# Laying out SBUF pools so that tiles read by TensorE begin at multiples of 2 KB

## The chip, the cores and the metric

One core of a Trainium2 chip runs the whole program. The metric is the device time of one execution in microseconds (us). TensorE (PE) does the matmuls, with its weight loads shown apart (PEld); VectorE (DVE), ScalarE (ACT) and GpSimd (POOL) do the elementwise work; SyncE (SP) issues the DMAs.

## The reference, cut to what matters

Two decoder layers over 512 positions of width 1024, all in float32. Layer 0 mixes positions by trailing means, layer 1 by differential attention over keys and values shared from the stream behind layer 0. Both end in a gated feed-forward network with a causal convolution of three taps:

```
for i in (0, 1):
    if i == 0: x = x + multiscale_pool(rmsnorm(x, norm_g[0, 0]), pool_w, pool_scale)
    else:
        k, v = rmsnorm(x, kv_norm) @ w_kv          # 1024 x (1024 + 1024)
        x = x + diff_attention(rmsnorm(x, norm_g[1, 0]), wq, lam, subln_g, wo, k, v)
    u = causal_dwconv(rmsnorm(x, norm_g[i, 1]) @ w_up[i], conv_w[i], conv_b[i])   # 1024 x 5632
    a, g = split(u)
    x = x + (silu(g) * a) @ w_down[i]              # 2816 x 1024
return rmsnorm(x, final_norm)
```

The two feed-forward networks are the bulk of it.

## The kernel before, in words

Every large product keeps float32 accuracy by splitting both operands into a high part (rounded to the type float32r) and a low part (the rest), and adding three matmuls of 128 x 128 weights: high by high, high by low, low by high. This is `mm3`, lines 158, 159 and 160, so each product shows as three lines of the profile. In a matmul the stationary operand (the 128 columns that are loaded as weights) is named second in a row of the trace, the moving operand (the 128, 256 or 512 columns that stream through) first: `pu<-n1h,hi_u` streams `n1h` through weights `hi_u`.

The products, by the name of their PSUM tile:

- `pu`, the up product of a feed-forward network: stationary a 128-column slice of a weight chunk (`hi_u`, `lo_u`), moving 512 positions of the normed and transposed stream (`n1h`, `n1l`; `n3h`, `n3l` in layer 1). The first four chunks of each layer are done in two halves of 256 positions each.
- `pd`, the down product: stationary a slice of the activations (`ah`, `al`), moving half a weight chunk (`hi_d`, `lo_d`).
- `pv`, the values: stationary the stream `n2`, moving half a weight chunk. `pw`, the output projection: stationary the heads' output, moving half a weight chunk.
- `pj_q`, `pj_k`, queries and keys: stationary a slice of a weight chunk, moving the stream `n2`.
- `pp`, the pooling maps: stationary the differences (`dhi`, `dlo`), moving 256 columns of a pooling weight.
- `sc`, `po`, `pa`, `pt`, `dps`: scores, weighted values, transposes and pooling bands.

SBUF is cut into pools that lie end to end in the order in which they are opened: `const` (residual stream `x`, gains, identity), `wp` (weight chunks: 3 raw, 5 high, 5 low buffers of 4 KB per partition), `work` (scratch, small vectors, loaded rows), `hp` (the normed stream, two buffers of 16 KB), `tp` (44 buffers of 2 KB: bands, pooling weights, activations, queries, keys, values). Where a pool begins is thus set by the sizes of those before it. In the built program the tiles that TensorE reads begin at these offsets from a multiple of 2048 bytes in their partition:

| tiles | before |
|---|---|
| `wp`: weight chunks, raw, high and low | 1984 |
| `hp`: `n1`, `n2`, `n3`, high and low | 1536 |
| `tp`: bands, pooling weights, `d`, `ah`, `al`, queries, keys, values, heads' output | 1536 |
| `work`: `aT`, `on` (2 KB scratch) | 1152 |
| `work`: `e`, `sq` (4 KB wide tiles) | 960 |
| `const`: identity | 1152 |

A slice adds its own start: 512 bytes for each 128 columns, 2048 for each 512. So a moving slice of `pu` begins at 1536, one of `pd` at 1984, and a stationary slice of `pu` 64 bytes ahead of a multiple of 512.

The instructions of TensorE stand in the order of the code (a manual schedule), and those of the other compute engines of the first 60 us too; `ORDER` is that list of steps. SP loads weight chunks ahead, as far as the raw buffers are free. `rows` loads a vector as rows of 128 into a tile of tag `vrow` (6 buffers), and `columns` turns them by a transpose on PE and a copy on DVE; step `c` of `ORDER` does that for the kv gain, the sub-norm gain and layer 0's convolution.

Of the kernel before, what the change touches and what calls it, by code (L numbers as in the profile page):

```python
# [8 lines left out]
F32 = mybir.dt.float32  # L9
# [5 lines left out]
P = 128  # L15
# [3 lines left out]
KD = D // P  # L19
# [44 lines left out]
def trunk(ctx, tc, x, norm_g, pool_w, pool_scale, kv_norm, w_kv, wq, lam, subln_g, wo,  # L64
          w_up, conv_w, conv_b, w_down, final_norm, consts, out):
    nc = tc.nc
    const = ctx.enter_context(tc.tile_pool(name="const", bufs=1))
    wp = ctx.enter_context(tc.tile_pool(name="wp", bufs=1))
    work = ctx.enter_context(tc.tile_pool(name="work", bufs=1))
    hp = ctx.enter_context(tc.tile_pool(name="hp", bufs=1))  # L70
    tp = ctx.enter_context(tc.tile_pool(name="tp", bufs=1))
    psum = ctx.enter_context(tc.tile_pool(name="psum", bufs=8, space=bass.MemoryType.PSUM))
    ctx.enter_context(tc.manual_schedule(engines={mybir.EngineType.PE}))

    def bank(name):
        return psum.tile([P, S], F32, tag="ps", name=name)
# [29 lines left out]
    nc.gpsimd.memset(halfneg, -0.5)  # L106

    def rows(src, n, name):
        r = work.tile([P, P], F32, tag="vrow", bufs=6, name=f"r_{name}")
        nc.sync.dma_start(out=r[:n, :], in_=src)  # L110
        return r, n, name

# [5 lines left out]
        return halves  # L118


    ones = const.tile([P, P], F32, name="ones")
    nc.vector.memset(ones, 1.0)

    def warm(n):
# [4 lines left out]
    load_x(0)  # L129
    nc.sync.dma_start(out=ident, in_=consts[:, :P])  # L130
    gn_rows = rows(norm_g.rearrange("l i (k p) -> (l i k) p", p=P), 4 * KD, "gn")
    nc.sync.dma_start(out=bands[0], in_=consts[:, P + S:P + 2 * S])
    load_x(1)
# [31 lines left out]
    def columns(loaded):  # L165

        r, n, name = loaded
        ps = bank(f"pv_{name}")
        nc.tensor.transpose(ps[:, :n], r[:n, :], ident[:n, :n])
        c = const.tile([P, n], F32, name=f"c_{name}")  # L170
        nc.vector.tensor_copy(c, ps[:, :n])
        return c
# [27 lines left out]
    class Normed:  # L200
# [13 lines left out]
        def vectors(self, t):  # L214
            self.rms(t)
            self.scale(t)
# [20 lines left out]
    def up_chunk(l, m):  # L237
        return chunk(w_up[l, :, m * P:(m + 1) * P].rearrange("(k p) c -> p k c", p=P), KD, P, f"u{l}_{m}")
# [6 lines left out]
    def conv_rows(l):  # L245
        return ([rows(conv_w[l, i].rearrange("(m p) -> m p", p=P), 2 * NF, f"cw{l}{i}") for i in range(3)]
                + [rows(conv_b[l].rearrange("(m p) -> m p", p=P), 2 * NF, f"cb{l}")])
# [12 lines left out]
    load_x(3)  # L260
    n1 = Normed("n1", across(norm_g[0, 1], "g1"))
    up0 = [up_chunk(0, (n + 1) % 2 * NF + n // 2) for n in range(2 * EARLY)]
    vec_rows = [rows(kv_norm.rearrange("(k p) -> k p", p=P), KD, "gkv"), rows(subln_g, 1, "gsub")]
    cw_rows = conv_rows(0)

    gn, shared, cw0 = [], [], []
# [75 lines left out]
        product(0, n, pup[n], up0[n][1:], n1, 0, S // 2)  # L342

    def vectors(_):
        shared.extend(columns(r) for r in vec_rows)
        cw0.extend(columns(r) for r in cw_rows)


# [1 line left out]
    steps = dict(a=pool_rms, h=pool_scaled, g=gains, m=pool_weights, x=pool_weights_split, i=pool_in,  # L350
                 s=pool_split, o=pool_out, r=pool_add, q=n1.rms, v=n1.scale, t=n1.turn, u=n1.split,
                 H=up_high, L=up_low, p=up_product, c=vectors, W=warm)
    with tc.manual_schedule(engines={mybir.EngineType.PE, mybir.EngineType.Activation,
                                     mybir.EngineType.DVE, mybir.EngineType.Pool}):
# [69 lines left out]
    def to_n2(t, dh):  # L424
# [3 lines left out]
        if t > 1:  # L428
# [2 lines left out]
    ffn(0, n1, cw0, [w[1:] for w in up0], pup, to_n2)  # L431


    gkv, gsub = shared
    gq = gn[0][:, 2 * KD:3 * KD]
    nc.vector.tensor_scalar(gsub, gsub, 1.0 - LAM_INIT, None, ALU.mult)
    lamt = scratch("lamt")
# [1 line left out]
                      in_=lam.rearrange("l a b -> l (a b)").to_broadcast([P, 4 * HD]))  # L439
# [318 lines left out]
```

## Time and profile before

| what | value |
|---|---|
| runs | 1019.69, 1019.77, 1018.54 us; median 1019.69 |
| profiled execution | 1019.51 us, its span 1017.7 us |
| PE busy | 1003.3 us, 99% |
| DVE busy, ACT busy | 56%, 42% |
| DMA | mean 94 GB/s, 8 tenths busy in the first fortieth of the span, 4 or less in all others |
| granted clock of TensorE | 0.998 of full speed over the span |

A matmul's time in a row is that of its passage through the engine; in the timeline the next begins before it ends. What a stream of matmuls costs is the distance from one start to the next, read from the timeline of PE.

### The profile page before, as it was taken

What the parts mean: (1) busy time and instruction counts of PE and PEld (TensorE: products, weight loads), DVE (VectorE), ACT (ScalarE), POOL (GpSimd) and SP (SyncE); (2) the same over time, 40 slices, a digit from 0 to 9 for tenths busy, and PEclk for the clock granted to TensorE, in tenths of its full rate; (3) what the DMA queues carried; (4) which work ended last, traced back from release to release, by engine and by line L of the source; (5) the groups of instructions that cost most, each with busy time, mean ns of one, the idle gap of its engine ahead of it and who ended that gap; (6) DMA issues with size and microseconds to landing.
All of it is one profiled execution on the core that took longest, in us unless ns stands there. A gap on an engine that the chain in (4) does not pass through costs nothing.

```text
span 1017.7 us, 12343 instructions
## 1 busy us (share of the span) xinstructions
PE 1003.3 (99%) x4871; PEld 835.6 (82%) x4871; DVE 569.5 (56%) x873; ACT 427.1 (42%) x671; POOL 86.1 (8%) x113
## 2 busy tenths in 40 slices
PE   8999999999999999999999999999999999999997
PEld 7998888888888888878888887988888888888885
DVE  5766656656632223457866797675665665622213
ACT  5554444443431213446756662454344443421311
POOL 3500000000000001261220101000000000000001
PEclk9999999999999999999999999999999999999999
DMA  8333333233232321243213111243333233232212
GB/s 256 108 104 104 90 97 103 85 102 104 83 109 84 113 88 57 79 129 104 63 42 104 63 43 42 83 125 104 91 96 104 85 102 104 83 104 85 102 42 82
DMA packets 128707, 95.33 MB, mean 94 GB/s; under 512 B 3329, under 2 KB 111498, under 8 KB 128650
## 3 DMA queue, kind: packets, MB, share of 16 engines
q1 hardware_dynamic: 128650, 94.55, 30.3%
q8 instruction: 38, 0.62, 0.3%
q14 instruction: 19, 0.16, 0.0%
HBM read 92.44 MB, written 2.10 MB: 93 GB/s over the span
## 4 chain that ended last, share of the span: by engine, by line
PE 97%; DVE 1%; DMA 1%; issue 0%; SPq 0%; ACT 0%; DVEq 0%; POOLq 0%; POOL 0%; ACTq 0%
PE pu L158 16%; PE pu L159 16%; PE pu L160 16%; PE pd L160 8%; PE pd L158 8%; PE pd L159 8%; PE sc L527 2%; PE po L556 2%; PE pw L160 1%; PE pv L158 1%; PE pv L160 1%; PE pv L159 1%; PE pj_k L159 1%; PE pj_k L158 1%; PE pw L159 1%; PE pw L158 1%
## 5 line engine op out<-in xcount | busy, mean ns | idle before, releaser
L141 DVE TENSOR_TENSOR lo_u<-raw_u,hi_u 128x1024 fp32r<-128x1024 f32 x84 | 103.3, 1232 | 130.3 <-ACT hi_u L140 130.2
L158 PE MATMUL pu<-n1h,hi_u 128*128 128x512 f32 (+1 forms) x384 | 144.1, 375 | 0.0
L159 PE MATMUL pu<-n3l,hi_u 128*128 128x512 f32 (+1 forms) x384 | 144.0, 375 | 0.0
L158 PE MATMUL pu<-n3h,hi_u 128*128 128x512 f32 (+1 forms) x384 | 143.6, 374 | 0.0
L160 PE MATMUL pu<-n1h,lo_u 128*128 128x512 f32 (+1 forms) x384 | 143.3, 373 | 0.0
L160 PE MATMUL pu<-n3h,lo_u 128*128 128x512 f32 (+1 forms) x384 | 142.1, 370 | 0.0
L159 PE MATMUL pu<-n1l,hi_u 128*128 128x512 f32 (+1 forms) x384 | 142.0, 370 | 0.0
L141 DVE TENSOR_TENSOR lo_d<-raw_d,hi_d 128x1024 fp32r<-128x1024 f32 x44 | 53.9, 1225 | 152.7 <-ACT hi_d L140 152.7
L158 PE MATMUL pd<-hi_d,ah 128*128 128x512 f32 x352 | 138.8, 394 | 0.0
L159 PE MATMUL pd<-lo_d,ah 128*128 128x512 f32 x352 | 138.7, 394 | 0.0
L160 PE MATMUL pd<-hi_d,al 128*128 128x512 f32 x352 | 138.7, 394 | 0.0
L140 ACT CAST hi_u<-raw_u 128x1024 fp32r<-128x1024 f32 x84 | 88.0, 1050 | 67.8 <-PE pu L159 62.9
L140 ACT CAST hi_d<-raw_d 128x1024 fp32r<-128x1024 f32 x44 | 46.1, 1048 | 148.0 <-PE pd L160 136.5
L158 PEld LDWEIGHTS pu<-n3h,hi_u 128*128 128x128 f32 x384 | 72.1, 188 | 14.1
L160 PEld LDWEIGHTS pu<-n1h,lo_u 128*128 128x128 f32 x384 | 72.1, 188 | 14.1
L160 PEld LDWEIGHTS pu<-n3h,lo_u 128*128 128x128 f32 x384 | 72.1, 188 | 13.4
L159 PEld LDWEIGHTS pu<-n1l,hi_u 128*128 128x128 f32 x384 | 72.1, 188 | 13.4
L158 PEld LDWEIGHTS pu<-n1h,hi_u 128*128 128x128 f32 x384 | 72.2, 188 | 12.0
L159 PEld LDWEIGHTS pu<-n3l,hi_u 128*128 128x128 f32 x384 | 72.2, 188 | 11.9
L160 PEld LDWEIGHTS pd<-hi_d,al 128*128 128x128 f32 x352 | 65.8, 187 | 16.4
L159 PEld LDWEIGHTS pd<-lo_d,ah 128*128 128x128 f32 x352 | 65.8, 187 | 16.3
L158 PEld LDWEIGHTS pd<-hi_d,ah 128*128 128x128 f32 x352 | 65.8, 187 | 16.1
(149 smaller groups left out, 1554.3 us busy)
## 6 DMA issues: line engine op xcount, KB each, us to landing
raw_u<-in_w_up_dram SPq DMA_DIRECT2D x88, 512.0 KB, 3.8
raw_d<-in_w_down_dram SPq DMA_DIRECT2D x44, 512.0 KB, 3.3
raw_v<-in_w_kv_dram SPq DMA_DIRECT2D x8, 512.0 KB, 3.6
raw_q<-in_wq_dram SPq DMA_DIRECT2D x8, 512.0 KB, 4.0
raw_k<-in_w_kv_dram SPq DMA_DIRECT2D x8, 512.0 KB
raw_o<-in_wo_dram SPq DMA_DIRECT2D x8, 512.0 KB, 5.1
x<-in_x_dram SPq DMA_DIRECT2D x4, 512.0 KB
out_dram<-y SPq DMA_DIRECT2D x8, 256.0 KB, 2.1
```

The costliest lines, as they stand in the source:

```text
L140: nc.scalar.copy(hi, src)
L141: nc.vector.tensor_tensor(lo, src, hi, ALU.subtract)
L158: nc.tensor.matmul(ps, lh, rh, start=first, stop=False)
L159: nc.tensor.matmul(ps, lh, rl, start=False, stop=False)
L160: nc.tensor.matmul(ps, ll, rh, start=False, stop=last)
L527: nc.tensor.matmul(ps[:, :m], qs[h, c][:, q], k[:, :m], start=not last, stop=bool(last))
L556: nc.tensor.matmul(po[h][:, qi * P:(qi + 1) * P], aT[:, kt * P:(kt + 1) * P], vt[kt][h // 4][:, (h % 4) * VD:(h % 4 + 1) * VD], start=kt = ...
```

## The change

The pools are opened in another order: a small pool `start` of 896 bytes, which holds `ones` (widened to 224 columns, of which 128 are used), then `tp`, `hp`, `wp`, `const`, `work`. `tp`, `hp` and `wp` hold whole multiples of 2 KB, so all of their tiles, and the identity, now begin at a multiple of 2048 bytes; `aT` and `on` begin at offset 1024, `e` and `sq` at 832. To make room `vrow` has 5 buffers, and the sub-norm gain is loaded as a ninth row under the eight of the kv gain, so that one transpose and one copy serve both.

```diff
-    const = ctx.enter_context(tc.tile_pool(name="const", bufs=1))
-    wp = ctx.enter_context(tc.tile_pool(name="wp", bufs=1))
+    start = ctx.enter_context(tc.tile_pool(name="start", bufs=1))
+    tp = ctx.enter_context(tc.tile_pool(name="tp", bufs=1))
+    hp = ctx.enter_context(tc.tile_pool(name="hp", bufs=1))
+    wp = ctx.enter_context(tc.tile_pool(name="wp", bufs=1))
+    const = ctx.enter_context(tc.tile_pool(name="const", bufs=1))
     work = ctx.enter_context(tc.tile_pool(name="work", bufs=1))
-    hp = ctx.enter_context(tc.tile_pool(name="hp", bufs=1))
-    tp = ctx.enter_context(tc.tile_pool(name="tp", bufs=1))
+    ones = start.tile([P, 224], F32, name="ones")
...
-        r = work.tile([P, P], F32, tag="vrow", bufs=6, name=f"r_{name}")
+        r = work.tile([P, P], F32, tag="vrow", bufs=5, name=f"r_{name}")
...
-    ones = const.tile([P, P], F32, name="ones")
+    ones = ones[:, :P]
...
-    vec_rows = [rows(kv_norm.rearrange("(k p) -> k p", p=P), KD, "gkv"), rows(subln_g, 1, "gsub")]
+    vec_rows = rows(kv_norm.rearrange("(k p) -> k p", p=P), KD, "gkv")
+    nc.sync.dma_start(out=vec_rows[0][KD:KD + 1, :], in_=subln_g)
...
-        shared.extend(columns(r) for r in vec_rows)
+        shared.append(columns((vec_rows[0], KD + 1, "gkv")))
...
-    gkv, gsub = shared
+    gkv, gsub = shared[0][:, :KD], shared[0][:, KD:]
```

The instructions of every engine stand in the same order as before, with the same shapes, but for one transpose on PE and one copy on DVE that are gone. On PE, at step `c` (some 40 us into the span), before; `pv_gkv`, `pv_gsub`, `pv_cw`, `pv_cb` are the transposed rows of the kv gain, the sub-norm gain and the convolution's taps and bias:

```order
176 L160 MATMUL pu_2_499<-n1h,lo_u_23_125 128x256
177 L169 MATMUL pv_gkv<-ident,r_gkv 128x8
178 L169 MATMUL pv_gsub<-ident,r_gsub 128x1
179 L169 MATMUL pv_cw_538<-ident,r_cw_135 128x44
180 L169 MATMUL pv_cw_542<-ident,r_cw_137 128x44
181 L169 MATMUL pv_cw_546<-ident,r_cw_139 128x44
182 L169 MATMUL pv_cb_550<-ident,r_cb_141 128x44
183 L158 MATMUL pu_0_560<-n1h,hi_u_22_116 128x256
```

And the same place of PE now:

```order
176 L163 MATMUL pu_2_501<-n1h,lo_u_23_128 128x256
177 L172 MATMUL pv_gkv<-ident,r_gkv 128x9
178 L172 MATMUL pv_cw_536<-ident,r_cw_137 128x44
179 L172 MATMUL pv_cw_540<-ident,r_cw_139 128x44
180 L172 MATMUL pv_cw_544<-ident,r_cw_141 128x44
181 L172 MATMUL pv_cb_548<-ident,r_cb_143 128x44
182 L161 MATMUL pu_0_558<-n1h,hi_u_22_119 128x256
```

The transpose of one column is gone and the one ahead of it has nine columns; all else stands as it stood. SP issues as many DMAs as before: the sub-norm gain's still follows the kv gain's.

## Rows read from the trace of the kernel before

**Rows 1.** Page, span and busy time of TensorE with its share and instructions

```profile
span 1017.7 us, 12343 instructions
...
PE 1003.3 (99%) x4871; PEld 835.6 (82%) x4871; DVE 569.5 (56%) x873; ACT 427.1 (42%) x671; POOL 86.1 (8%) x113
```

**Rows 2.** Page, chain of work that ended last, shares by engine

```profile
PE 97%; DVE 1%; DMA 1%; issue 0%; SPq 0%; ACT 0%; DVEq 0%; POOLq 0%; POOL 0%; ACTq 0%
```

**Rows 3.** Groups by line and form, whole span: count | busy us, mean ns | idle

```profile
L158 PE MATMUL pd<-hi_d,ah 128*128 128x512 f32 x352 | 138.8, 394 | 0.0
...
L158 PE MATMUL pu<-n1h,hi_u 128*128 128x512 f32 x320 | 126.1, 394 | 0.0
...
L158 PE MATMUL pw<-hi_o,oh 128*128 128x512 f32 x64 | 25.8, 404 | 0.8 <-ACT oh L145 0.8
L158 PE MATMUL pv<-hi_v,n2h 128*128 128x512 f32 x64 | 25.5, 399 | 0.0
...
L158 PE MATMUL pj_q<-n2h,hi_q 128*128 128x512 f32 x64 | 25.1, 393 | 0.0
...
L158 PE MATMUL pu<-n3h,hi_u 128*128 128x256 f32 x64 | 18.1, 284 | 0.0
```

**Rows 4.** Groups by line and form, weight loads of the down product

```profile
L158 PEld LDWEIGHTS pd<-hi_d,ah 128*128 128x128 f32 x352 | 65.8, 187 | 16.1
```

**Rows 5.** Timeline of PE, up product of layer 0: start us, passage us, engine, line

```profile
99.76 0.39 PE L159 MATMUL pu<-n1l,hi_u 128*128 128x512 f32 x1
...
119.67 0.39 PE L159 MATMUL pu<-n1l,hi_u 128*128 128x512 f32 x1
```

**Rows 6.** Timeline of PE, down product of layer 0

```profile
299.68 0.39 PE L158 MATMUL pd<-hi_d,ah 128*128 128x512 f32 x1
...
319.98 0.39 PE L158 MATMUL pd<-hi_d,ah 128*128 128x512 f32 x1
```

**Rows 7.** Timeline of PE, values and output projection

```profile
420.53 0.39 PE L160 MATMUL pv<-hi_v,n2l 128*128 128x512 f32 x1
...
429.63 0.39 PE L160 MATMUL pv<-hi_v,n2l 128*128 128x512 f32 x1
...
627.49 0.39 PE L158 MATMUL pw<-hi_o,oh 128*128 128x512 f32 x1
...
633.79 0.39 PE L158 MATMUL pw<-hi_o,oh 128*128 128x512 f32 x1
```

**Rows 8.** Timeline of PE, queries and keys, two stretches

```profile
434.76 0.40 PE L158 MATMUL pj_q<-n2h,hi_q 128*128 128x512 f32 x1
...
451.56 0.40 PE L158 MATMUL pj_k<-n2h,hi_k 128*128 128x512 f32 x1
...
468.09 0.39 PE L158 MATMUL pj_q<-n2h,hi_q 128*128 128x512 f32 x1
...
472.21 0.39 PE L158 MATMUL pj_q<-n2h,hi_q 128*128 128x512 f32 x1
```

**Rows 9.** Timeline of PE, matmuls of 256 columns, four stretches

```profile
30.62 0.28 PE L158 MATMUL pp<-pwh,dhi 128*128 128x256 f32 x1
...
32.42 0.28 PE L158 MATMUL pp<-pwh,dhi 128*128 128x256 f32 x1
...
37.40 0.28 PE L158 MATMUL pu<-n1h,hi_u 128*128 128x256 f32 x1
...
39.78 0.28 PE L158 MATMUL pu<-n1h,hi_u 128*128 128x256 f32 x1
...
41.25 0.28 PE L158 MATMUL pu<-n1h,hi_u 128*128 128x256 f32 x1
...
45.84 0.28 PE L158 MATMUL pu<-n1h,hi_u 128*128 128x256 f32 x1
...
52.19 0.28 PE L158 MATMUL pu<-n1h,hi_u 128*128 128x256 f32 x1
...
60.67 0.28 PE L158 MATMUL pu<-n1h,hi_u 128*128 128x256 f32 x1
```

## The prediction, made before the changed kernel was run

> **What bounds the kernel now.** I read the page first: PE is busy 1003.3 of 1017.7 us [rows 1], and the chain of work that ended last is 97% PE [rows 2]. So nearly every nanosecond by which PE's stream of matmuls is shortened or stretched goes into the time, and what the other engines do has room: DVE is at 56%, ACT at 42%. Next I counted the matmuls by form [rows 3]: each row there is one of the three lines of a split product, so the down product has 3 x 352 = 1056 matmuls of 512 columns, the up products 6 x 320 = 1920 (three lines in each of two layers) and 6 x 64 = 384 of 256 columns, values and output projection 3 x 64 = 192 each, queries and keys 6 x 64 = 384. The mean durations in these rows (394 ns) are passages that overlap, and say nothing of the rate. So last I read starts in the timeline, and divided the distance of two of them by the matmuls between.
>
> That gives the observation on which all rests: matmuls of one shape come at different distances, each very steadily.
> - Up product: 19.91 us for 87 matmuls, 228.9 ns each [rows 5].
> - Down product: 20.30 us for 87, 233.3 ns [rows 6].
> - Values 9.10 us for 39, output projection 6.30 us for 27: both 233.3 ns [rows 7].
> - Queries and keys: 16.80 us for 72, 233.3 ns, in their first stretch, and 4.12 us for 18, 228.9 ns, later [rows 8].
> - With 256 columns: pooling maps 1.80 us for 15, 120.0 ns; up product 2.38 us for 21, 113.3 ns, in the first chunk, then 4.59 us for 39, 117.7 ns, and 8.48 us for 72, 117.8 ns [rows 9].
> No row shows PE waiting inside these stretches. The weights of a matmul are loaded in 187 ns [rows 4], less than either distance at 512 columns, so there the load has some 40 ns of cover.
>
> **The change part by part.** The order of work stays. Removed are one transpose of a single row with its copy, on PE less than two distances of 0.12 us; I cost them at nothing. The fifth `vrow` buffer instead of a sixth, with one tile fewer to hold, leaves the bias rows waiting for the same release as before, and PE has other products queued then: nothing. The DMAs are as many and as large. DVE, ACT and POOL do the same shapes at other addresses; if one of them slowed by some per cent, its 44% or more of idle time would take it up.
>
> What is left is where the operands of 3744 matmuls of 512 columns, and of the smaller ones, begin. Before, kinds with the moving operand in `hp` begin 1536 bytes past a multiple of 2048, which is a multiple of 512; those whose moving operand is a weight chunk begin 64 bytes short of a multiple. The first kinds are the up product and queries and keys, the second the down product, values and output projection. This is the same cut as between 228.9 and 233.3, but for the first stretch of queries and keys, which follows the values in the order and keeps their distance. I take the moving start as the cause: the moving operand is four times the bytes of the weights here, and the weights are covered. After the change every moving operand of 512 columns begins at a multiple of 512 (and of 2048).
>
> So the forecast is that all of them run at the up product's distance:
> - down product, values, output projection: 1056 + 192 + 192 = 1440 matmuls by 4.4 ns: 6.3 us less;
> - the first stretch of queries and keys: the 72 of [rows 8] and some 24 beside them by 4.4 ns: 0.4 us less;
> - up products, the rest of queries and keys, 256 columns: unchanged.
> The sum is 6.7 us, against the profiled execution of 1019.51 us (a span of 1017.7 and 1.8 around it): 1012.8 us. The median of the runs is 1019.69, so the profiled one stands for them; I say 1013.
>
> The effect of a start at a multiple of 2048 itself is shown by no row, and I bound it. Below: if the 113.3 ns of the first chunk is what a free stream of 256 columns costs, 512 cost no more than two, 226.6 ns; this is the gain's end by rows. Above: if two matmuls of the pooling maps are the measure, 240 ns, and the 3744, each at its own distance now, lose 6.7 or 11.1 ns: 1440 x 6.7 + 1920 x 11.1 + some 4 = 35 us, a time of 1055. I take the value of the up product, since it is the nearest row: same columns, same weights' shape, longest steady stretch. That a stream inside crosses a multiple of 2048 costs nothing that I can see: first halves of 256 columns cross one (from 1536 to 2560), second halves don't (2560 to 3584), and they run at 117.7 and 117.8 [rows 9]. So no gain is booked for that, though the change ends all such crossings.
>
> [...]
>
> **The rivals.**
> *The stationary start decides, and it gets slower.* All kinds at 233.3 have stationary slices that begin at a multiple of 512; the up product and the later queries and keys, at 228.9, have theirs 64 bytes off. The pooling maps begin both operands at multiples of 512, as everything will after the change, and are slow among those of 256 columns: 120.0 against 117.7, and the distance fell to 113.3 when the up product followed them with no break between [rows 9]. That is the strongest evidence against my forecast. Against it: at 256 columns the load of 187 ns is longer than the distance, so it is not covered as at 512; and the first queries and keys ran at 233.3 with stationary slices 64 bytes off. Price: 1920 up matmuls by 4.4 ns are 8.5 us, 288 queries and keys 1.3 us, 384 of 256 columns by 2.3 ns 0.9 us; 1019.5 + 10.7 = 1030.2 us. It decides from the point where the up product alone loses 3.3 ns, which eats the 6.3 us of the others.
>
> *More is gained than the up product's distance.* The 113.3 ns show that a better distance exists; if operands that both begin at 2048 hold it, 512 columns cost 226.6: 1440 x 6.7 + 1920 x 2.3 + 384 x about 3 + 360 x 4.4 ns = 9.6 + 4.4 + 1.2 + 1.6 = 16.8 us, a time of 1002.7; more if a part of what all rows share goes too. For it speaks that one chunk of one shape and placement ran so; against it that three others of the same placement did not, nor the second half of the same chunk.
>
> *Placement has no part.* The same placement ran at 233.3 and 228.9 for queries and keys, at 113.3 and 117.7 for the up product; what ran before seems to matter, and the order is unchanged. Then the time is 1019.5. Against it: of the five kinds of 512 columns four keep one distance, and it goes by their placement [rows 5 to 8]; values and queries are products of the same build, 24 matmuls into one PSUM tile, and differ in where the operands lie. Gains and losses of the first two rivals could also cancel here.
> [...]
>
> **How the numbers follow.** Forecast 0.36, at 1011 to 1015; slower through the stationary start 0.33; more gained 0.17; no part 0.14. Under 0.2%, some 2 us, a time can't be told from no change here. Faster is the forecast, nearly whole, and the third: 0.51. Same: 0.15. Slower: 0.34. For 8 in 10 the range must hold the rival on the other side up to 1032 and the smaller form of the larger gain, from 995 on; left out are its larger forms and the 1055 of the upper bound.
>
> **What would show it.** Right: in the timeline the down product comes at 228.9 ns, as the up product. Stationary start: the up product at 233.3 and the pooling maps unchanged. More gained: up product under 228, 256 columns at 113.3. No part: every distance as now. The forecast is wrong if the up product's distance moves at all, for by it the up product is already where the change brings the rest.

## The result, and the profile after

The changed kernel takes 1008.41 us (median of 6 runs, 1006.30 to 1012.28), the kernel before on the same chip 1019.60 (6 runs): a ratio of 0.9896, 95% interval 0.9874 to 0.9917. The time lies in the range that was forecast, on the side that was forecast, but 4.6 us below the 1013 of the likeliest case and outside the 1011 to 1015 that were given to it. The profiled execution took 1007.95 us.

The page after, span and busy time:

```profile
span 1006.2 us, 12339 instructions
...
PE 991.4 (99%) x4870; PEld 838.3 (83%) x4870; DVE 569.7 (57%) x872; ACT 426.9 (42%) x671; POOL 85.7 (9%) x113
```

DVE, ACT and POOL are busy as long as before [rows 1] to within 0.5 us; PE is busy 11.9 us less, and the span is 11.5 us shorter. PE's timeline shows where. The up and the down product of layer 0 after (start us, passage us, engine, line; lines stand 3 lower in this kernel, so 161 to 163 are 158 to 160):

```profile
99.82 0.39 PE L162 MATMUL pu<-n1l,hi_u 128*128 128x512 f32 x1
...
119.54 0.39 PE L162 MATMUL pu<-n1l,hi_u 128*128 128x512 f32 x1
...
299.74 0.39 PE L162 MATMUL pd<-lo_d,ah 128*128 128x512 f32 x1
...
319.46 0.39 PE L162 MATMUL pd<-lo_d,ah 128*128 128x512 f32 x1
```

Both need 19.72 us for 87 matmuls: 226.7 ns, where it was 228.9 [rows 5] and 233.3 [rows 6]. Values, and queries and keys in their first stretch, in the same view:

```profile
417.71 0.39 PE L162 MATMUL pv<-lo_v,n2h 128*128 128x512 f32 x1
...
426.56 0.39 PE L162 MATMUL pv<-lo_v,n2h 128*128 128x512 f32 x1
...
435.85 0.39 PE L161 MATMUL pj_k<-n2h,hi_k 128*128 128x512 f32 x1
...
448.77 0.39 PE L161 MATMUL pj_q<-n2h,hi_q 128*128 128x512 f32 x1
```

8.85 us for 39 and 12.92 for 57: 226.9 and 226.7 ns, where both were 233.3 [rows 7, 8]. With 256 columns, the pooling maps, then the up product's first chunk and the next:

```profile
30.25 0.28 PE L161 MATMUL pp<-pwh,dhi 128*128 128x256 f32 x1
...
31.69 0.28 PE L161 MATMUL pp<-pwh,dhi 128*128 128x256 f32 x1
...
36.67 0.28 PE L161 MATMUL pu<-n1h,hi_u 128*128 128x256 f32 x1
...
39.19 0.28 PE L161 MATMUL pu<-n1h,hi_u 128*128 128x256 f32 x1
...
41.35 0.28 PE L161 MATMUL pu<-n1h,hi_u 128*128 128x256 f32 x1
...
45.67 0.28 PE L161 MATMUL pu<-n1h,hi_u 128*128 128x256 f32 x1
```

12, 21 and 36 matmuls, all at 120.0 ns. The pooling maps stayed where they were; the up product came from 113.3 and 117.7 [rows 9] and is slower. So in these stretches each shape has one distance now, and the two shapes went opposite ways.

The waits of PE after (who waited for whom: us in total, times, longest) have one line that the trace of before did not have:

```profile
PE pv L163 <- DVE n2l L144: 1.9, 1, 1.9
```

### The profile page after: what moved, and what is told of

Its sections match the earlier page's. It is cut to its first block, busy times and chain, and to the rows that moved or that the text cites. A ratio compares the mean times of both kernels' runs of the same rounds, so it can differ in the third digit from the quotient of the medians.

```text
span 1006.2 us, 12339 instructions
## 1 busy us (share of the span) xinstructions
PE 991.4 (99%) x4870; PEld 838.3 (83%) x4870; DVE 569.7 (57%) x872; ACT 426.9 (42%) x671; POOL 85.7 (9%) x113
## 4 chain that ended last, share of the span: by engine, by line
PE 96%; DVE 1%; DMA 1%; ACT 0%; issue 0%; SPq 0%; POOL 0%; DVEq 0%; POOLq 0%; ACTq 0%
PE pu L161 16%; PE pu L162 16%; PE pu L163 16%; PE pd L163 8%; PE pd L161 8%; PE pd L162 8%; PE sc L531 2%; PE po L560 2%; PE pw L163 1%; PE pj_k L161 1%; PE pj_k L162 1%; PE pw L162 1%; PE pw L161 1%; PE pj_k L163 1%; PE pj_q L162 1%; PE pj_q L161 1%
```

## The experiments

A convention for all of them: the *difference* of a kind of matmul is its moving start minus its stationary start in bytes, taken modulo 256. Before the change it was 64 for the up product, queries and keys, 192 for the down product, values and output projection, 0 for the pooling maps; after it, it is 0 for all of these.

**1. The weight pool at its old start.** Pools opened as `wp`, a gap of 64 bytes, `tp`, `hp`:

```diff
+    wp = ctx.enter_context(tc.tile_pool(name="wp", bufs=1))
+    pad0 = ctx.enter_context(tc.tile_pool(name="pad0", bufs=1))
+    gap0 = pad0.tile([P, 16], F32, name="gap0")
...
-    wp = ctx.enter_context(tc.tile_pool(name="wp", bufs=1))
...
-    ones = start.tile([P, 224], F32, name="ones")
+    ones = start.tile([P, 208], F32, name="ones")
```

> Of the changed kernel only the weight pool moves: its chunks begin 1984 bytes past a multiple of 2048, as before the change; the stream (hp) and the activations (tp) stay at multiples of 2048. Three theories. M, the moving start decides: up product, queries and keys (moving in hp) stay at 226.7 ns, down product, values and output projection (moving in wp) go back to 233.3, some 1440 x 6.7 = 9.6 us, 1018. S, the stationary start decides: up product, queries and keys go to 228.9 (2300 x 2.2 = 5 us), the 256-column ones back to 117.8 (0.8 us less), the down product stays at 226.7, 1012.5. R, the two starts against each other decide: both go back to the distances before, 228.9 and 233.3, and the time is near 1019.

1020.19 us, a ratio of 1.0009 to before (0.9996 to 1.0022): the whole gain is gone. Timeline, up and down product:

```profile
99.62 0.39 PE L164 MATMUL pu<-n1l,hi_u 128*128 128x512 f32 x1
...
119.53 0.39 PE L164 MATMUL pu<-n1l,hi_u 128*128 128x512 f32 x1
...
299.77 0.39 PE L164 MATMUL pd<-lo_d,ah 128*128 128x512 f32 x1
...
319.37 0.39 PE L164 MATMUL pd<-lo_d,ah 128*128 128x512 f32 x1
```

19.91 us for 87 are 228.9 ns, 19.60 for 84 are 233.3: the distances of before, although the stream in `hp` begins at a multiple of 2048 here. Of the three theories of the expectation M and S each miss one of the two; R has both. That the moving start of the up product is 0 or 1536 past a multiple of 2048 makes no difference: 228.9 ns in both.

**2. The stream alone at 1984.** The same edit with `hp` first, then the gap, `tp`, `wp`.

> Only the normed stream (hp) begins at 1984; weights and activations stay at multiples of 2048. M: up product, queries and keys (their moving operand) go to 233.3 ns, 2304 x 6.7 = 15.4 us, 1024; all else stays. S: only the values (hp is their stationary operand) go to 228.9, 192 x 2.2 = 0.4 us, 1009. R: both, 1024 with the values at 228.9.

1021.96 us, 1.0021 of before (1.0007 to 1.0036).

```profile
99.61 0.39 PE L163 MATMUL pu<-n1h,hi_u 128*128 128x512 f32 x1
...
119.21 0.39 PE L163 MATMUL pu<-n1h,hi_u 128*128 128x512 f32 x1
...
427.48 0.39 PE L163 MATMUL pv<-hi_v,n2h 128*128 128x512 f32 x1
...
431.60 0.39 PE L163 MATMUL pv<-hi_v,n2h 128*128 128x512 f32 x1
```

Up product 19.60 us for 84, 233.3 ns; values, whose stationary operand it is, 4.12 for 18, 228.9. Again R. The time is 2 us below R's 1024; the 256-column products, which R's sum had left at 120, ran at a mean of 117 ns in this trace. Of their 16 groups of 24, all at a difference of 192, eight came at 113.3 ns and eight at 117.8.

**3. The activations alone at 1984.** `tp` first, then the gap, `hp`, `wp`.

> Only tp (activations, heads' output, pooling weights and differences, queries and keys for the scores) begins at 1984. M: down product, output projection and up product stay at 226.7 ns, time as after the change, 1008.4; the pooling maps, whose moving operand is there, get slower than 120. S and R: down product and output projection, whose stationary operand is there, go to 228.9, 1248 x 2.2 = 2.8 us, 1011; the pooling maps, both of whose operands move alike, stay at 120.0 by R.

1010.05 us, 0.9904 of before (0.9881 to 0.9927). The down product's stationary operand is moved, its moving one is not:

```profile
299.78 0.39 PE L165 MATMUL pd<-hi_d,al 128*128 128x512 f32 x1
...
319.69 0.39 PE L165 MATMUL pd<-hi_d,al 128*128 128x512 f32 x1
```

19.91 us for 87: 228.9 ns. M falls. The pooling maps, both of whose operands moved by the same, kept 120 as their commonest distance, as R has it. The time alone, 1.6 us above the changed kernel, would not have told M from R.

**4. Starts against starts, matmuls alone.** The layers are left out; only a copy of x and streams of 24 matmuls are left:

```diff
...
+        for j in range(24):
+            k = j // 6
+            a, b = m // 4 + k * S, s // 4 + k * P
+            nc.tensor.matmul(ps[:, :n], stat[:, b:b + P], mov[:, a:a + n], start=j == 0, stop=j == 23)
...
```

> The disputed cost alone: none of the layers is computed; the kernel copies x out, and PE runs 24 matmuls in float32r for each pair of a moving start (0, 64, 128, 256, 512, 1024, 1536, 1984 bytes past a multiple of 2048) and a stationary start (0, 64, 128, 256, 448), first with 512 columns, then with 256, with four small float32 matmuls between the pairs. M: the distance goes by the moving start alone, 226.7 ns at 0, 228.9 at 512, 1024 and 1536, 233.3 at 64 and 1984. S: by the stationary start alone. R: by the difference of both. If 2 KB is the step that counts, moving starts of 512, 1024 and 1536 are slower than 0; if 512 bytes is, they are alike. Where before a kind had two distances, what ran just before it counts, and the map will show no order.

Two of the 80 streams in the timeline, stationary starts 64 and 256 with moving start 0, each with the small matmuls behind it:

```profile
19.38 5.84 PE L50 MATMUL m<-mov,stat 128*128 128x512 f32 x24
25.06 1.05 PE L43 MATMUL b<-ones 128*128 128x128 f32 x8
...
32.33 5.72 PE L50 MATMUL m<-mov,stat 128*128 128x512 f32 x24
37.90 1.06 PE L43 MATMUL b<-ones 128*128 128x128 f32 x8
```

From the start of a stream to the first small matmul it is 5.68 us in the one and 5.57 in the other. The first matmuls of a stream don't have its steady distance yet (224 to 241 ns in experiment 10), so the table takes the mean of the last twelve distances of each stream, all from one execution. The 40 pairs of either width fall into four classes by the difference:

| difference | pairs with 512 columns | with 256 columns |
|---|---|---|
| 0 | 226.7 ns (all but the first stream of the program, 230.2: it lies in the second fortieth of the span, where the page shows a granted clock of 7 tenths of full speed, against 9 in all others) | 120.0 |
| 64 | 228.8 to 228.9 | 117.8 |
| 128 | 232.6 to 233.3 | 118.8 to 119.0 |
| 192 | 233.3 | 113.3, one 117.8 |

Moving starts of 0, 256, 512, 1024 and 1536 give the same rows to 0.1 ns. So neither 2 KB nor 512 bytes is the step: R holds with a period of 256 bytes, and M and S are out. At a difference of 192 the 256 columns have two distances, as in experiment 2; which of them comes is not settled here.

**5. Finer steps**, the same kernel with stationary starts in steps of 16 bytes, moving starts 0 and 32, and 384 columns besides.

> Matmuls alone, none of the layers is computed. Moving start 0 or 32 bytes past a multiple of 2048, stationary start in steps of 16 bytes up to 256, and 4, 8 and 60; with 512, 384 and 256 columns. R with a period of 256 bytes (what the run before showed): with 512 columns 226.7 ns at a difference of 0 and of 256, 233.3 where the stationary start is 64 ahead, 228.8 where it is 192 ahead; with 256 columns 120.0, 113.3 and 117.8; and moving 32 against stationary 32 + s gives what 0 against s gives. If steps of 64 bytes are all that counts, 4 to 60 read as 0, 80 to 112 as 64. If finer steps count there are values between, perhaps below 226.7. 384 columns: near 175, the lowest where 512 has its lowest.

No pair with 512 columns came below 226.7. Moving start 0 against 0, 64, 192 and 256 repeat 226.7, 233.3, 228.8 and 226.7. In between there is no rule that I can read: 0 against 16, 32 and 48 has 233.3, against 240 has 226.7; 32 against 16, 32 and 48 has 226.7, against 64 has 233.3; 4 and 8 give 232.4 and 230.4. My guess that steps below 64 read as 0 is wrong, and so is the guess that only the difference counts at that grain. 384 columns lie between 173.0 and 180.0 ns with no order. With 256 columns 0 against 0, 192 and 256 have 120.0, 117.8 and 120.0, as above, but 0 against 64 has 117.8 where experiment 4 had 113.3. For layouts in steps of 64 bytes the table above stands at 512 columns.

**6. Everything at 1984.** `start` of 208 columns and no gap: `tp`, `hp`, `wp` and the identity all begin 64 bytes short of a multiple of 2048.

```diff
-    ones = start.tile([P, 224], F32, name="ones")
+    ones = start.tile([P, 208], F32, name="ones")
```

> The changed kernel with all three pools, and the identity, begun at 1984: no tile that TensorE reads begins at a multiple of 2048, nor of 512, but all differences are as after the change. R: all distances as after the change, 226.7 and 120.0 ns, time the same, 1008.4 within 0.3%. M or S, or 2 KB multiples as such: 512 columns at 228.9 to 233.3, 3744 matmuls by 2.2 to 6.7 ns, 1016 to 1033.

1007.48 us, 0.9877 of before (0.9856 to 0.9899). Up product:

```profile
99.82 0.39 PE L162 MATMUL pu<-n1l,hi_u 128*128 128x512 f32 x1
...
119.54 0.39 PE L162 MATMUL pu<-n1l,hi_u 128*128 128x512 f32 x1
```

19.72 us for 87, 226.7 ns, as with multiples of 2048. The gain needs no tile at a multiple of 2 KB; it needs the operands to agree.

**7. The rest of the change alone.** The kernel before with the joined gain rows and five row buffers, and a place-holding tile of 512 bytes ahead of `hp`, so that every start is the old one.

```diff
...
+    gap = ctx.enter_context(tc.tile_pool(name="gap", bufs=1))
+    held = gap.tile([P, P], F32, name="held")
...
```

> The kernel before with the rest of the change alone: one transpose for both gains and five row buffers, with a tile that only holds place, so that every tile TensorE reads begins where it began before. All theories: as before, within 0.1%, and the distances 228.9, 233.3, 113.3 to 120.0 as before. If it is faster by more than 0.2%, part of the gain isn't due to where tiles begin.

1018.94 us, 0.9993 of before (0.9983 to 1.0002): no gain that can be told; in its trace the up and the down product come at 228.9 and 233.3 ns, as before. But it has a line that the trace of before lacks:

```profile
PE pv L162 <- DVE n2l L143: 1.4, 1, 1.4
```

So the wait of the values comes at the old starts too, and where tiles begin isn't shown to bring it. The traces of the changed kernel, of experiments 1 to 3, 6 and 9, and this one have it (1.2 to 1.9 us); all have the joined rows and five buffers, and the one trace without them has not. Whether that part of the change brings it, or it differs from one execution to another, is open.

**8. That wait taken away.** In the changed kernel, behind the down product of layer 0:

```diff
-        n2.vectors(t)
         if t > 1:
             n2.tensors(t - 2)
+        n2.vectors(t)
```

> The changed kernel with the two steps behind the down product in the other order: the transposes and the split of the normed stream of a tile stand ahead of the scaling of a later one, on DVE too. In the trace of the changed kernel PE waits 1.9 us for that split behind a scaling that takes 2.5 us. If the wait is part of what the change brought, or at least sits on the path, 2 us less than the changed kernel on the same chip, and no wait of the values for n2l; if something else is as late, no difference.

**9. The changed kernel on the same chip.**

> The changed kernel again, to compare with the one before this on one chip: 1006 to 1012 us; its spread is that of the wait for n2l, 0 to 4 us, if that wait differs from one execution to another.

Experiment 8 took 1004.41 us (1003.92 to 1006.00), experiment 9 1006.74 (1006.50 to 1007.91); 0.9861 (0.9845 to 0.9877) and 0.9884 (0.9866 to 0.9902) of before. The four runs of each don't overlap, and the medians are 2.3 us apart. DVE in the trace of the changed kernel, where the wait ends:

```profile
407.33 2.12 DVE L199 TENSOR_SCALAR sq_n<-x,r_n 128x512 f32<-128x512 f32 x1
409.37 1.28 DVE L144 TENSOR_TENSOR n2l<-pt_n,n2h 128x512 fp32r<-128x512 f32 x2
```

and in experiment 8:

```profile
403.96 1.28 DVE L144 TENSOR_TENSOR n2l<-pt_n,n2h 128x512 fp32r<-128x512 f32 x2
...
406.29 2.52 DVE L199 TENSOR_SCALAR sq_n<-x,r_n 128x512 f32<-128x512 f32 x2
```

The split of one tile had stood in DVE's queue behind the scaling of a later one; ahead of it, it is done before PE comes for it, and its trace shows no wait of the values for `n2l`. This is the fastest of all versions here. In experiment 9 the wait was 1.7 us, near the 1.9 of the first trace; that its size makes the spread of the runs (6 us in the first set, 1.4 here) is not shown.

**10. One difference right behind another**, matmuls alone again, with no break between the two streams of a pair.

```diff
...
+                stream(n, 512, 512 - was)
+                stream(n, 512, 512 - then)
...
```

> Matmuls alone, none of the layers is computed. 24 matmuls at one difference of moving and stationary start (0, 64, 128, 192 bytes), then with no break 24 at another, all 16 pairs, with 512 and with 256 columns, four small float32 matmuls ahead of each pair. If the difference alone decides, the second stretch has the distance of its own difference whatever stood ahead: 226.7, 228.8, near 233, 233.3. If what ran before counts too, as the first stretch of queries and keys before the change had it, a difference of 64 has 233.3 behind a difference of 192 and 228.8 behind itself; and 256 columns at 64 have 113.3 behind 0 and 117.8 behind the small matmuls.

Mean of the last twelve distances of the second stream, again from one execution:

| then | 512 columns, behind 0 / 64 / 128 / 192 | 256 columns, behind 0 / 64 / 128 / 192 |
|---|---|---|
| 0 | 226.7 / 226.7 / 226.7 / 226.7 | 120.0 / 120.0 / 120.0 / 120.0 |
| 64 | 228.9 / 228.8 / 228.9 / 233.3 | 113.3 / 117.8 / 117.8 / 113.3 |
| 128 | 232.6 / 232.6 / 233.3 / 231.7 | 118.3 / 119.0 / 118.4 / 118.8 |
| 192 | 233.3 / 233.3 / 233.3 / 233.3 | 117.8 / 117.8 / 117.8 / 117.8 |

Both oddities of the trace before are in it: a difference of 64 runs at 233.3 behind 192, as the first queries and keys did behind the values [rows 8], and at 113.3 with 256 columns behind 0, as the first up chunk did behind the pooling maps [rows 9]. At a difference of 0 what ran before no longer shows in the last twelve distances. It does in the first ones: up to some ten matmuls behind another stream, here and in the changed kernel's queries and keys behind the scores, came at 224 to 241 ns. With 256 columns a difference of 192 is not settled by what ran just before: as the first stream of a pair, each time behind the small matmuls, it came twice at 113.3 and twice at 117.8.

## Why the prediction was right, and where it was not

The bound and the direction were right. The mechanism was not: 6.7 us less were forecast, nearly all from the down product, the values and the output projection, and the medians differ by 11.2, to which the up product gave what it was not to give. So it is in part luck that the time fell into the range.

*What bounds the kernel* held: PE's distances went into the time nearly whole. By the steady ones, 1440 matmuls by 6.7 ns are 9.6 us, 1920 by 2.2 are 4.2, queries and keys 108 x 6.7 + 276 x 2.2 ns = 1.3 (their first stretch was 108 matmuls long, 12 more than the prediction counted); against them 256 columns, 360 x 2.2 + 24 x 6.7 ns = 1.0, and the wait of 1.9. That is 12.2 us, and the span fell by 11.5. Summed from start to start over the whole of both traces, the down product fell by 7.0 us, the up product with 512 columns by 4.2, queries and keys by 0.9 and the output projection by 0.8; the values rose by 1.15, with the wait in it, and the 256 columns by 0.9; all else fell by 0.6. So values, output projection, queries and keys gave less than their steady distances say, for their first matmuls behind other work come slower (up to 241 ns in queries and keys behind the scores).

*The removed transpose, the row buffers, the DMAs and the other engines at nothing*: right for the time, by experiment 7.

*"I take the moving start as the cause"*: wrong. Experiments 1 to 3 show that neither start decides alone, and 4 that the two modulo 256 bytes do. The cut in the trace was real, but the kinds differed in both operands at once, and the rows with both at a multiple of 512, the pooling maps, I set aside because their loads (190 ns each in the trace of before) are longer than their distance (120.0). They were the rows to trust for 256 columns: all of these went to their 120.0.

*Down product, values and output projection by 4.4 ns, 6.3 us*: the sign was right and the size too small. They gained 6.7 ns at best, since their difference went to 0 and not to the up product's 64.

*"Up products ... unchanged"*: wrong on both sides, 2.2 ns less at 512 columns and 2.3 to 6.7 more at 256. The prediction named a moving up product as what would refute it, and so it did: the time came out right by the third case, *more is gained*, at its 226.6 ns, less what the 256 columns lost and the wait. That its bound, two matmuls of 113.3, met 226.7 is chance: 256 columns at that placement take 120.0. That a part of what all rows share could go too was a guess of mine: no pair that was tried came below 226.7 at 512 columns.

*The stationary start decides* was right that what begins alike runs as the pooling maps at 256 columns (120.0 ns), and wrong at 512, where the like starts are the fastest (226.7).

*Placement has no part*: out, by experiments 1 to 4: the start of one operand against the other moved the distance by up to 6.7 ns, from 226.7 to 233.3 at 512 columns and from 113.3 to 120.0 at 256. Where in TensorE's path the time is lost no run here shows. What spoke for this rival, two distances at one placement, is explained by what ran before, as experiment 10 shows.

*Crossing a multiple of 2048 costs nothing*: right; in experiment 4 moving starts of 0 and 1536 give the same to 0.1 ns, 226.7 at a difference of 0.

The 1.9 us wait was in no step. Whether the change brings it is open, as experiment 7 says.

## What to carry to other kernels

Where PE bounds a kernel, read its matmuls' distance from the starts in the timeline, by kind; where one shape has two, look at where both operands begin, and compare them modulo 256 bytes. For float32r with 512 columns let them agree: layouts of tiles in multiples of 256 bytes gave 226.7 ns, begun at a multiple of 2048 and 64 bytes short of one (experiment 6); a tile of 64 bytes between two pools undid it, for the products whose operands lie on both sides of it (228.9 and 233.3 ns, experiments 1 to 3). With 256 columns agreeing starts were the slowest of the four classes, 120.0 ns. When two causes run together in every row, a forecast from one of them is a guess, and a kernel of bare matmuls over all pairs settles it in one run.

## What the runs showed of the hardware that I had not expected

- The distance of float32r matmuls goes by moving against stationary start modulo 256 bytes, for starts in steps of 64: 226.7 to 233.3 ns at 512 columns, 113.3 to 120.0 at 256, with the best at 512 (difference 0) the slowest at 256.
- At differences of 64 and 128 bytes what ran just before can set the distance to the end of a stream of 24 matmuls (with 512 columns 64: 233.3 behind 192, 228.8 behind itself; 128: 231.7 behind 192, 233.3 behind itself), and in the kernel before for over 70 [rows 8]. At 192 with 256 columns there are two distances, 113.3 and 117.8, and what chooses is not shown. A difference of 0 came to 226.7 and 120.0 behind every other stream that was tried, at 512 columns within some ten matmuls (up to 241 ns till then).
- No pair tried came below 226.7 ns at 512 columns.
